# Latent attention: operands split before they are stored, softmax division on ScalarE, and layer 0's memory weights split on VectorE

## The chip, the cores and the metric

One NeuronCore of one Trainium2 chip. The metric is the device time of one execution of the whole kernel in microseconds (us), as a median over several executions. Engines: TensorE (PE, its weight loads PEld), VectorE (DVE), ScalarE (ACT), GpSimd (POOL), and SyncE (SP), which in this kernel only issues DMAs. "Granted clock" is the share of full speed that TensorE was allowed.

## What is computed

A decoder trunk of two layers on 1024 tokens of width 1024, all float32. Each layer is a mixer, a cross-attention into 256 memory tokens and a squared-ReLU MLP, each between two RMS norms and added to the residual. Layer 0's mixer, in which the change lies, computes two groups of heads from one input projection:

```python
def _mla(c_q, c_kv, k_pe, positions, g_q, w_uq, g_kv, w_ukv):      # 8 heads
    q = (_rmsnorm(c_q, g_q) @ w_uq).reshape(B, S, H, 64 + 32)      # rank 256
    kv = (_rmsnorm(c_kv, g_kv) @ w_ukv).reshape(B, S, H, 64 + 64)  # rank 128
    q_pe, k_pe = rope(q[..., 64:]), rope(k_pe)                     # k_pe is shared by the heads
    s = (q_nope @ k_nope.T + q_pe @ k_pe.T) * (64 + 32) ** -0.5    # causal
    o = softmax(s) @ v
...
def _gla(q, k, v, g_lr, r, w_gate, b_gate, g_norm):                # 4 heads, 64 and 128 wide
    # S_t = diag(a_t) S_{t-1} + k_t^T v_t, o_t = q_t S_t, in chunks
    o = _rmsnorm(o, g_norm).reshape(B, S, H * DV)                  # over each head's 128
    return o * silu(r)
...
mix = concat(mla, gla) @ w_out
```

The cross-attention's keys and values come from the memory tokens and four weight matrices of each layer (`xa_w_k`, `xa_w_v`, `xa_w_q`, `xa_w_o`).

## The kernel before

**Products.** Each float32 operand of a matmul is split into a high half, rounded to TensorE's fast format (fp32r), and a low half, the rest; `acc3` adds three products: high by high, high by low, low by high. `split` makes the halves: by default ScalarE copies the high half (line 137), VectorE or, with `lo_eng="pool"`, GpSimd subtracts it from the source for the low half (line 143). `fetch` loads a weight block of 128x1024 into `raw` and splits it into `wh` and `wl`; a `Stream` fetches a list of blocks some blocks ahead.

**Stages.** Layer 0's mixer (`mix0`) has the input projection, then the latent projections, in two groups of four heads (`grp`), then eight token tiles of the gate `r` (`tok`), then the attention. For each group the latent projections compute, feature by feature:
- `qpe`, the rotary part of the four queries (`uq`, evicted by ScalarE at line 1207), which eight DMAs from SBUF to SBUF copy with halves exchanged into `swap` (line 1209); VectorE multiplies both with cosine and sine, GpSimd adds, and four DMAs store the result to `mq` in DRAM (line 1214);
- for both pairs of heads `q` and `k` (lines 1220 and 1223), stored head by head to `mq` and `mk` (lines 1225 and 1226), in plain float32;
- `v` for eight token tiles (line 1234), stored to `mv` for each four tiles (line 1237).

**The attention** sweeps 8 heads by 4 blocks of 256 queries (`seq`). For a step, `scores` computes two tiles of 128 queries: matmuls, the row maximum (VectorE, line 1302), the exponential with its row sum (ScalarE, 1304), the reciprocal and the division (VectorE, 1305 and 1306), into `prob`. `turn` transposes `prob` on TensorE and splits the transposes; `values` multiplies them with V. `head_qk` loads a head's `q` and `k` (three DMAs) into `raw` buffers and splits them, `pair_v` does so for V, ahead of use. Into the gaps between the matmuls the code writes two other streams of work, one after each step: the gated linear attention, a generator (`gla`), chunk by chunk: gate levels `lev`, Gram products `gr`, state update `gS`, output `o`, its norm (lines 1036 to 1042), the transpose `gT` and the store to `gd`; and layer 0's memory stage (`mem_side`), which folds the 32 blocks of cross-attention weights with the memory.

**Order and buffers.** A scheduler writes the order of each engine from the code's order when the kernel is built. Each engine works its list in order, SP too; SP's DMAs take turns on 8 semaphores. Buffers are tiles of fixed pools: 34 of 128x1024 (`u`), 12 for weights, 3 `raw`, 3 `t2`; in PSUM single banks (`p1`) and double banks (`p2`). A buffer is given again when its last reader is done: for a tile that is stored, when the store has landed.

Of the kernel before, what the change touches and what calls it, by code (L numbers as in the profile page):

```python
# [77 lines left out]
class Trunk:  # L78
# [635 lines left out]
    def mem_side(self, l):  # L714
# [7 lines left out]
        W = Stream(self, blocks, 1, "pool")  # L722
# [158 lines left out]
    def mix0(self):  # L881
# [11 lines left out]
        ggla = self.cp.tile([P, P], F32, name="ggla")  # L893
        nc.sync.dma_start(ggla, self.bcast_row(T["g_gla"]))
# [6 lines left out]
        qd, kd = self.dram("mq", [8, 96, S]), self.dram("mk", [8, 64, S])  # L901
        krd, vd = self.dram("mkr", [32, S]), self.dram("mv", [4, P, NT, P])
# [27 lines left out]
        def gla():  # L930
# [6 lines left out]
            for c in range(NT):  # L937
# [99 lines left out]
                nc.vector.tensor_tensor(natural(oc), heads(o[:, :, 0:256]), natural(srg), ALU.mult)  # L1037
                nc.vector.tensor_reduce(stt[:, 0:4], at.rearrange("p r (a b) -> p (r a) b", b=P), AX.X, ALU.add)
                self.rstd(stt[:, 4:8], stt[:, 0:4])
                for hd in range(4):  # L1040
                    w, x = slice(hd * P, (hd + 1) * P), 4 + 2 * (hd % 2) + hd // 2
                    nc.vector.tensor_scalar(oc[:, w], oc[:, w], stt[:, x:x + 1], None, ALU.mult)
# [19 lines left out]
        def head_qk(hd):  # L1062
            res = []
            for a in range(2):
                t = self.raw([P, S], "qk")
                if a:
                    nc.sync.dma_start(t[0:64, :], kd[hd])
                    nc.sync.dma_start(t[64:96, :], krd)
                else:
                    nc.sync.dma_start(t[0:96, :], qd[hd])  # L1070
                h, l = self.parts([96, S], "kq"[1 - a])
                self.split(h, l, t[0:96, :])
                res.append((h, l))
            qk[hd] = res

        def pair_v(pair):
            t = self.raw([P, NT, P], "V")
            nc.sync.dma_start(t.rearrange("p a b -> p (a b)"), vd[pair].rearrange("p a b -> p (a b)"))

            V[pair] = [self.u([P, NT, 2, 64], F32R, "V") for _ in range(2)]  # L1080
            for b, x in enumerate(V[pair]):
                self.split(x[:, :, 0, :], x[:, :, 1, :], t[:, :, 64 * b:64 * b + 64])


        with self.psum(4, 2):
# [56 lines left out]
            nc.sync.dma_start(krd, kr[0:32, :])  # L1142
            del pe, kr, wg, reset, c0
# [52 lines left out]
            for grp in range(2):  # L1196
                wuq = self.fetch(T["w_uq"][grp])

                def uq(t, half):
                    ps = self.p1("uq")  # L1200
                    self.acc3(ps, [(tuple(w[:, t * 256 + k * P:t * 256 + k * P + P] for w in wuq), tuple(x[:, half_cols(half)] for x in qn[k])) for k in range(2)])
                    return ps


                x, y = self.u([P, S], F32, "qpe"), self.u([P, S], F32, "swap")
                for half in range(2):
                    nc.scalar.activation(x[:, half_cols(half)], uq(0, half), AF.Copy, scale=asc)
                for h in range(8):
                    nc.sync.dma_start(y[16 * h:16 * h + 16, :], x[16 * (h ^ 1):16 * (h ^ 1) + 16, :])
                nc.vector.tensor_tensor(x, x, cs, ALU.mult)  # L1210
                nc.vector.tensor_tensor(y, y, sn, ALU.mult)
                nc.gpsimd.tensor_tensor(x, x, y, ALU.add)
                for h in range(4):
                    nc.sync.dma_start(qd[4 * grp + h, 64:96, :], x[32 * h:32 * h + 32, :])
                for pair in range(2 * grp, 2 * grp + 2):
                    q, k = self.u([P, S], F32, "q"), self.u([P, S], F32, "k")
                    w = slice(pair * P, pair * P + P)
                    for half in range(2):
                        c = half_cols(half)
                        nc.scalar.activation(q[:, c], uq(1 + pair % 2, half), AF.Copy, scale=asc)  # L1220
                        ps = self.p1("uk")
                        self.acc3(ps, [(tuple(x[:, w] for x in wkv), tuple(x[:, c] for x in kn))])
                        nc.vector.tensor_copy(k[:, c], ps)
                    for b in range(2):
                        nc.sync.dma_start(qd[2 * pair + b, 0:64, :], q[64 * b:64 * b + 64, :])
                        nc.sync.dma_start(kd[2 * pair + b], k[64 * b:64 * b + 64, :])
                w = slice(512 + grp * 256, 512 + grp * 256 + 256)
                for i in range(NT):
                    if not i % 4:
                        v = self.u([P, 4, 2, P], F32, "v")  # L1230
                    ps = self.p1("V")
                    t = slice(i * P, (i + 1) * P)
                    self.acc3(ps[:, :256], [(tuple(x[:, t] for x in kn), tuple(x[:, w] for x in wkv))])
                    nc.scalar.activation(v[:, i % 4], ps[:, :256].rearrange("p (a b) -> p a b", a=2), AF.Copy)
                    if i % 4 == 3:
                        for a in range(2):
                            nc.sync.dma_start(vd[2 * grp + a][:, i - 3:i + 1, :], v[:, :, a, :])
            del wuq, wkv, qn, kn, x, y, q, k, v, cs, sn
            self.rope = None
            wv = [W.next() for _ in range(4)]  # L1240
            for i in range(NT):
                x = self.t2()
                self.silu(x, tok(i, wv), self.t2())
                v = x.rearrange("p (a b) -> p a b", b=P)
                nc.gpsimd.tensor_tensor(v, v, ggla.unsqueeze(1).broadcast_to([P, 4, P]), ALU.mult)
# [7 lines left out]
            del wv, x, v  # L1253
# [11 lines left out]
        with self.psum(4, 2):  # L1265
# [10 lines left out]
            def scores(hd, r):  # L1276
# [3 lines left out]
                for a in range(2):  # L1280
# [25 lines left out]
                    nc.vector.tensor_scalar(p, p, st[:, 3:4], None, ALU.mult)  # L1306
                    pts.append(p)
                probs[hd, r] = pts

            def turn(hd, r):  # L1310
# [3 lines left out]
                for jp in range(r + 1):  # L1314
# [3 lines left out]
                    for n, (jj, a) in enumerate(cells):  # L1318
                        nc.tensor.transpose(tp[:, n * P:n * P + P], pts[a][:, (2 * jp + jj) * P:(2 * jp + jj + 1) * P], self.ident)
# [7 lines left out]
            def values(hd, r):  # L1327
                xs = probs.pop((hd, r))
                b, pair = hd % 2, hd // 2
                v = V[pair][b]  # L1330
                po = self.p1("pv")
                n = 2 * r + 2
                for j in range(n):
# [37 lines left out]
            values(*seq[-2])  # L1371
            turn(*seq[-1])
# [451 lines left out]
def pack(inputs):  # L1824
# [53 lines left out]
    A["g_gla"] = f["ev_g_gla"]  # L1878
# [62 lines left out]
```

## Time and profile before

| | |
|---|---|
| median of 3 executions | 2979.53 us (2977.46 to 2980.94) |
| profiled execution: its own time, its span | 2979.67 us, 2977.9 us |
| mean granted clock | 0.980 |
| busy share of the span: PE, PEld, DVE, ACT, POOL | 96, 79, 64, 47, 30% |
| DMA | 385.09 MB, mean 129 GB/s |

The span runs from the first to the last recorded instruction; the own time has a little around it. A row of a timeline begins with its start and its length in us, then the engine, the line of the kernel, the operation, output<-inputs with shapes, and a count; in square brackets stands the time for which the engine was idle before it and what ended that. A row of a group ends with its busy time, the mean ns of one, and the idle time before its members by what ended it. Busy shares are means over stages with different limits, so a stage is read from its own stretch.

### The profile page before, as it was taken

To read this page: it belongs to the slowest core of one execution; us is meant where nothing else is said; L and a number is where in the kernel's file an instruction comes from. 1 tells how busy PE (TensorE), PEld (TensorE's weight loads), DVE (VectorE), ACT (ScalarE), POOL (GpSimd) and SP (SyncE) were. 2 spreads that over 40 slices of the span, in tenths; PEclk is the share of its full clock that TensorE was granted. 3 is DMA by queue.
4 is the path that set the end of the run, shared out by engine and by line. 5 is a ranking of instruction groups with operands and counts; after the bars stand their busy time and mean duration, and the time that the engine had idled before them with its cause. 6 is when DMAs were issued, how large, how long until landed. Compare 5 with 4: busy or idle time off the path is not lost. (4 is left out here: it accounts for less than half of the span.)

```text
span 2977.9 us, 37928 instructions
## 1 busy us (share of the span) xinstructions
PE 2846.6 (96%) x14470; PEld 2355.4 (79%) x14470; DVE 1909.4 (64%) x2348; ACT 1402.7 (47%) x2391; POOL 898.2 (30%) x674
## 2 busy tenths in 40 slices
PE   7998999999999999999999999889999999999998
PEld 6777888888887888787867888887788788878776
DVE  4237788754347443799876657887733744458995
ACT  4346666633346455433445565543433655544332
POOL 2204545233330000167050113357533100006723
PEclk9998999999999999999999999999999999999999
DMA  4264544352322333531163345547323233263204
GB/s 160 97 165 147 168 141 148 116 197 71 109 104 90 109 113 136 203 114 64 52 223 96 122 144 178 189 163 251 113 63 121 85 108 112 103 231 111 98 17 142
DMA packets 165222, 385.09 MB, mean 129 GB/s; under 512 B 16748, under 2 KB 66316, under 8 KB 165040
## 3 DMA queue, kind: packets, MB, share of 16 engines
q1 hardware_dynamic: 146608, 349.10, 35.0%
q10 hardware_dynamic: 18432, 33.56, 2.9%
q8 instruction: 114, 1.87, 0.3%
q14 instruction: 68, 0.56, 0.1%
HBM read 267.86 MB, written 113.69 MB: 128 GB/s over the span
## 5 line engine op out<-in xcount | busy, mean ns | idle before, releaser
L143 DVE TENSOR_TENSOR wl<-blk,wh 128x1024 fp32r<-128x1024 f32 x276 | 451.7, 1659 | 320.0 <-ACT wh L137 320.0
L493 POOL TENSOR_TENSOR blk<-blk 128x1024 f32<-128x1024 f32 x80 | 252.4, 3183 | 869.0 <-DVE wl L143 863.5
L137 ACT ACTIVATE wh<-blk 128x1024 fp32r<-128x1024 f32 x276 | 281.8, 1054 | 327.6 <-PE op L561 188.7
L560 PE MATMUL up<-hnh,wh 128*128 128x512 f32 x896 | 356.0, 398 | 9.6 <-ACT hnh L137 5.0
L561 PE MATMUL up<-hnl,wh 128*128 128x512 f32 x896 | 354.5, 396 | 4.8 <-DVE hnl L143 4.8
L562 PE MATMUL up<-hnh,wl 128*128 128x512 f32 x896 | 353.4, 395 | 0.0
L561 PE MATMUL op<-wl,wh 128*128 128x512 f32 x784 | 307.9, 393 | 9.7 <-DVE wl L143 9.6
L560 PE MATMUL op<-wh 128*128 128x512 f32 x784 | 306.3, 395 | 6.2 <-ACT wh L137 6.2
L562 PE MATMUL op<-wh,wl 128*128 128x512 f32 x784 | 306.0, 390 | 0.0
L137 ACT ACTIVATE wh<-raw 128x1024 fp32r<-128x1024 f32 (+1 forms) x163 | 170.6, 1058 | 138.1 <-DMA raw<-hd 25.9
L143 POOL TENSOR_TENSOR wl<-raw,wh 128x1024 fp32r<-128x1024 f32 x66 | 158.9, 2420 | 223.6 <-ACT wh L137 208.3
L560 PEld LDWEIGHTS up<-hnh,wh 128*128 128x128 f32 x896 | 169.1, 189 | 51.3 <-ACT hnh L137 11.4
L561 PEld LDWEIGHTS up<-hnl,wh 128*128 128x128 f32 x896 | 169.3, 189 | 45.5 <-DVE hnl L143 6.3
L562 PEld LDWEIGHTS up<-hnh,wl 128*128 128x128 f32 x896 | 169.3, 189 | 40.1
L143 DVE TENSOR_TENSOR wl<-raw,wh 128x1024 fp32r<-128x1024 f32 (+1 forms) x97 | 126.6, 1315 | 99.7 <-ACT wh L137 99.3
L561 PEld LDWEIGHTS op<-wl,wh 128*128 128x128 f32 x784 | 148.0, 189 | 47.1 <-DVE wl L143 16.4
L560 PEld LDWEIGHTS op<-wh 128*128 128x128 f32 x784 | 149.1, 191 | 39.0 <-ACT wh L137 8.2
L562 PEld LDWEIGHTS op<-wh,wl 128*128 128x128 f32 x784 | 147.8, 188 | 30.5
L187 POOL TENSOR_SCALAR st<-st 128x1 f32<-128x1 f32 x99 | 41.6, 421 | 361.6 <-ACT hn L303 307.4
L306 POOL TENSOR_TENSOR h<-h,hn 128x1024 f32<-128x1024 f32 x47 | 128.4, 2732 | 33.5 <-DVE hn L305 26.2
L673 DVE TENSOR_TENSOR acc<-acc,op 128x512 f32<-128x512 f32 x192 | 123.8, 676 | 4.3 <-PE op L562 4.1
L287 DVE SCALAR_TENSOR_TENSOR hn<-h,st,gain 128x1024 f32<-128x1024 f32 x48 | 101.8, 2122 | 26.1 <-POOL st L188 24.8
(440 smaller groups left out, 6993.5 us busy)
## 6 DMA issues: line engine op xcount, KB each, us to landing
blk<-in_ffn_w_dram SPq DMA_DIRECT2D x120, 512.0 KB, 4.3
h<-h SPq DMA_DIRECT2D x80, 512.0 KB, 4.1
hd<-t ACTq DMA_DIRECT2D x128, 256.0 KB, 2.9
blk<-hd SPq DMA_DIRECT2D x56, 512.0 KB, 4.2
raw<-in_w_in_dram SPq DMA_DIRECT2D x24, 512.0 KB, 4.1
h<-in_x_dram SPq DMA_DIRECT2D x16, 512.0 KB, 6.3
raw<-in_xa_w_k_dram SPq DMA_DIRECT2D x16, 512.0 KB, 3.7
raw<-in_xa_w_v_dram SPq DMA_DIRECT2D x16, 512.0 KB, 3.8
```

The source lines that it names most:

```text
L137: nc.scalar.activation(hi, src, AF.Copy)
L143: e.tensor_tensor(lo, src, hi.bitcast(F32), ALU.subtract)
L187: self.nc.gpsimd.tensor_scalar(dst, src, EPS, None, ALU.add)
L287: nc.vector.scalar_tensor_tensor(hn, h, st[:, 1:2], gpre, ALU.mult, ALU.mult)
L306: nc.gpsimd.tensor_tensor(h, h, t, ALU.add)
L493: eng.tensor_tensor(out, a, b, op)
L560: mm(ps, lh, rh, start=start and not i, stop=False, skip_group_check=True)
L561: mm(ps, lh, rl, start=False, stop=False, skip_group_check=True)
L562: mm(ps, ll, rh, start=False, stop=i == n - 1, skip_group_check=True)
L673: nc.vector.tensor_tensor(dst, dst, ps[i], ALU.add)
```

## The change

Four edits:
1. **Layer 0's memory weights**: the low halves of the 32 blocks are computed on VectorE and not on GpSimd.
2. **Operands split at their source**: `q`, `k`, `v`, the rotary parts and the shared rotary key are split where the projection is evicted, and both halves are stored (`mq`, `mk`, `mkr` and `mv` have twice the size); `q` and `k` in pieces of 512 tokens, `v` of two token tiles. `head_qk` and `pair_v` load the halves straight into `u` tiles, six DMAs for a head and two for a pair, without a split. The rotary products move from VectorE to GpSimd, and behind the group's V tiles.
3. **Division**: `divide` scales `prob` on ScalarE; the code calls it for a step ahead of the next step's `scores`.
4. **Linear attention's norm**: `o` is scaled by the norm and multiplied with the gate in one VectorE instruction for each head, from PSUM; the gain `g_gla` is a scale for each partition at the eviction of `gT` and no longer a product on GpSimd for each of the eight gate tiles.

```diff
-        W = Stream(self, blocks, 1, "pool")
+        W = Stream(self, blocks, 1, "pool" if l else "dve")
...
-                nc.vector.tensor_tensor(natural(oc), heads(o[:, :, 0:256]), natural(srg), ALU.mult)
                 nc.vector.tensor_reduce(stt[:, 0:4], at.rearrange("p r (a b) -> p (r a) b", b=P), AX.X, ALU.add)
                 self.rstd(stt[:, 4:8], stt[:, 0:4])
                 for hd in range(4):
...
-                    nc.vector.tensor_scalar(oc[:, w], oc[:, w], stt[:, x:x + 1], None, ALU.mult)
+                    nc.vector.scalar_tensor_tensor(oc[:, w], o[:, a, p * P:p * P + P], stt[:, x:x + 1], srg[:, w], ALU.mult, ALU.mult)
...
-                    nc.scalar.activation(g, tp, AF.Copy)
+                    nc.scalar.activation(g, tp, AF.Copy, scale=ggla)
...
         def head_qk(hd):
             res = []
             for a in range(2):
-                t = self.raw([P, S], "qk")
-                if a:
-                    nc.sync.dma_start(t[0:64, :], kd[hd])
-                    nc.sync.dma_start(t[64:96, :], krd)
-                else:
-                    nc.sync.dma_start(t[0:96, :], qd[hd])
-                h, l = self.parts([96, S], "kq"[1 - a])
-                self.split(h, l, t[0:96, :])
-                res.append((h, l))
+                res.append(self.parts([96, S], "kq"[1 - a]))
+                for part, t in enumerate(res[a]):
+                    if a:
+                        nc.sync.dma_start(t[0:64, :].bitcast(F32), kd[hd, part])
+                        nc.sync.dma_start(t[64:96, :].bitcast(F32), krd[part])
+                    else:
+                        nc.sync.dma_start(t.bitcast(F32), qd[hd, part])
...
-            V[pair] = [self.u([P, NT, 2, 64], F32R, "V") for _ in range(2)]
-            for b, x in enumerate(V[pair]):
-                self.split(x[:, :, 0, :], x[:, :, 1, :], t[:, :, 64 * b:64 * b + 64])
+            V[pair] = [self.u([P, 4, 2, 2, 64], F32R, "V") for _ in range(2)]
+            for t, src in zip(V[pair], vd[pair]):
+                nc.sync.dma_start(t.rearrange("p a b c d -> p (a b c d)").bitcast(F32), src.rearrange("p a b c d -> p (a b c d)"))
...
-                nc.vector.tensor_tensor(x, x, cs, ALU.mult)
-                nc.vector.tensor_tensor(y, y, sn, ALU.mult)
-                nc.gpsimd.tensor_tensor(x, x, y, ALU.add)
-                for h in range(4):
-                    nc.sync.dma_start(qd[4 * grp + h, 64:96, :], x[32 * h:32 * h + 32, :])
                 for pair in range(2 * grp, 2 * grp + 2):
-                    q, k = self.u([P, S], F32, "q"), self.u([P, S], F32, "k")
...
-                        nc.scalar.activation(q[:, c], uq(1 + pair % 2, half), AF.Copy, scale=asc)
+                        q, k = self.u([P, 2, HALF], F32R, "q"), self.u([P, 2, HALF], F32R, "k")
+                        ps = uq(1 + pair % 2, half)
+                        nc.scalar.activation(q[:, 0], ps, AF.Copy, scale=asc)
+                        nc.vector.scalar_tensor_tensor(q[:, 1], ps, asc, q[:, 0].bitcast(F32), ALU.mult, ALU.subtract)
...
-                        nc.vector.tensor_copy(k[:, c], ps)
-                    for b in range(2):
-                        nc.sync.dma_start(qd[2 * pair + b, 0:64, :], q[64 * b:64 * b + 64, :])
-                        nc.sync.dma_start(kd[2 * pair + b], k[64 * b:64 * b + 64, :])
+                        self.split(k[:, 0], k[:, 1], ps)
+                        for b in range(2):
+                            for t, dst in ((q, qd), (k, kd)):
+                                nc.sync.dma_start(dst[2 * pair + b, :, 0:64, c].rearrange("r p t -> p r t"), t[64 * b:64 * b + 64].bitcast(F32))
...
-                    nc.scalar.activation(v[:, i % 4], ps[:, :256].rearrange("p (a b) -> p a b", a=2), AF.Copy)
-                    if i % 4 == 3:
+                    self.split(v[:, i % 2, :, :, 0, :], v[:, i % 2, :, :, 1, :], ps[:, :256].rearrange("p (a b c) -> p a b c", a=2, b=2))
+                    if i % 2:
...
+                nc.gpsimd.tensor_tensor(x, x, cs, ALU.mult)
+                nc.gpsimd.tensor_tensor(y, y, sn, ALU.mult)
+                nc.gpsimd.tensor_tensor(x, x, y, ALU.add)
+                xs = self.parts([P, S], "qpe")
+                self.split(*xs, x, lo_eng="pool")
+                for part, t in enumerate(xs):
+                    for h in range(4):
+                        nc.sync.dma_start(qd[4 * grp + h, part, 64:96, :], t[32 * h:32 * h + 32, :].bitcast(F32))
...
-                nc.gpsimd.tensor_tensor(v, v, ggla.unsqueeze(1).broadcast_to([P, 4, P]), ALU.mult)
...
-                    nc.vector.tensor_scalar(p, p, st[:, 3:4], None, ALU.mult)
-                    pts.append(p)
+                    pts.append((p, st))
...
+            def divide(hd, r):
+
+                for p, st in probs[hd, r]:
+                    nc.scalar.activation(p, p, AF.Copy, scale=st[:, 3:4])
...
+                if n:
+                    divide(*seq[n - 1])
                 scores(hd, r)
```

How the order of the engines changes, at three places.

**ScalarE, latent projections of the second group.** `uq`, `uk` and `V` are PSUM banks; in brackets stand the semaphores for which a row waits (DMAHW0 to DMAHW7 are the DMAs' eight). Before:

```order
L1207 ACTIVATE qpe_1492<-uq_1494 128x512 [waits PE_49]
L1207 ACTIVATE qpe_1492<-uq_1502 128x512 [waits PE_49]
L1220 ACTIVATE q_1525<-uq_1527 128x512 [waits DMAHW5_49,DMAHW7_49,PE_49,Activation_49]
L1220 ACTIVATE q_1525<-uq_1540 128x512 [waits PE_49]
L1220 ACTIVATE q_1557<-uq_1559 128x512 [waits DMAHW2_49,DMAHW3_49,DMAHW1_49,DMAHW4_49,DMAHW0_49,DMAHW6_49,PE_49,Pool_49]
L1220 ACTIVATE q_1557<-uq_1572 128x512 [waits PE_49]
L1234 ACTIVATE v_1589<-V_1590 128x256 [waits DMAHW3_49,DMAHW4_49,DVE_49,PE_49]
```

and now:

```order
L1202 ACTIVATE qpe_1539<-uq_1541 128x512 [waits DMAHW1_49,DMAHW3_49,DVE_49,PE_49]
L1202 ACTIVATE qpe_1539<-uq_1549 128x512 [waits PE_49]
L1211 ACTIVATE q_1565<-uq_1567 128x512 [waits DMAHW4_49,DMAHW6_49,DVE_49,PE_49]
L137 ACTIVATE k_1566<-uk_1576 128x512 [waits DMAHW5_49,DMAHW7_49,DVE_49,PE_49]
L1211 ACTIVATE q_1586<-uq_1588 128x512 [waits DMAHW0_49,DMAHW1_49,DVE_49,PE_49]
L137 ACTIVATE k_1587<-uk_1597 128x512 [waits DMAHW2_49,DMAHW3_49,DVE_49,PE_49]
L1211 ACTIVATE q_1607<-uq_1609 128x512 [waits DMAHW4_49,DMAHW5_49,DVE_49,PE_49]
L137 ACTIVATE k_1608<-uk_1618 128x512 [waits DMAHW6_49,DMAHW7_49,DVE_49,PE_49]
L1211 ACTIVATE q_1628<-uq_1630 128x512 [waits DMAHW1_49,DMAHW2_49,DMAHW0_49,DMAHW3_49,PE_49,Pool_49]
L137 ACTIVATE k_1629<-uk_1639 128x512 [waits DMAHW6_49,DMAHW5_49,DMAHW7_49,DMAHW4_49,PE_49]
```

Each eviction of `q` and of `k` in the second group now takes a buffer of its own and waits for DMAs that read its old content, the last two for the stores of the first group's rotary halves.

**SP, from the last stores of the latent projections to the attention's first loads** (`grd` is the gate's tile, `cm` the causal mask, `G` the linear attention's first chunk, `gain` and `mem` belong to the memory stage). Before:

```order
L1237 DMA mv<-v 128x4x128 x2
L1214 DMA mq<-qpe 32x1024 x4
L1237 DMA mv<-v 128x4x128 x2
L1070 DMA qk<-mq 96x1024
L1067 DMA qk<-mk 64x1024
L1068 DMA qk<-mkr 32x1024
L1268 DMA cm<-in_cmask_dram 128x512
L720 DMA gain<-in_g_mem_dram 128x1024
L1246 DMA grd<-t_1647 128x512
L940 DMA G<-gld 128x1024
```

and now:

```order
L1230 DMA mv<-v 128x2x256 x8
L1238 DMA mq<-qpeh 32x1024 x4
L1238 DMA mq<-qpel 32x1024 x4
L1246 DMA grd<-t_1736 128x512
L1067 DMA qh<-mq 96x1024
L1067 DMA ql<-mq 96x1024
L1064 DMA kh<-mk 64x1024
L1065 DMA kh<-mkr 32x1024
L1064 DMA kl<-mk 64x1024
L1246 DMA grd<-t_1769 128x512
L1065 DMA kl<-mkr 32x1024
L936 DMA G<-gld 128x1024
```

A group's transfers from `swap` to the last store grow from 24 to 40 (8 swaps, 16 of `q` and `k`, 8 of `v`, 8 of the rotary halves). A head's six loads and two gate tiles' stores now stand between the last of them and `G`.

**VectorE, a late chunk of the linear attention in the attention** (at 420 us of the trace before; `t` is the chunk's output, `stg` its norm, `kt` the keys' halves, `sta` the maxima and sums of a step's rows, `pv` the values' bank). Before:

```order
L963 TENSOR_TENSOR lev<-lev,G 128x256 x4
L1042 TENSOR_SCALAR t_3962<-t_3962,stg 128x128
L1032 SCALAR_TENSOR_TENSOR gS<-gS,ekq,su 128x128 x2
L143 TENSOR_TENSOR kt<-kt 128x512
L1042 TENSOR_SCALAR t_3962<-t_3962,stg 128x128 x3
L1302 TENSOR_REDUCE sta<-sc 128x1 x2
L1305 RECIPROCAL sta<-sta 128x1
L1306 TENSOR_SCALAR prob<-prob,sta 128x896
L1344 TENSOR_TENSOR t_4024<-pv,t_4024 64x256
L1305 RECIPROCAL sta<-sta 128x1
L1306 TENSOR_SCALAR prob<-prob,sta 128x1024
```

and now:

```order
L959 TENSOR_TENSOR lev<-lev,G 128x256 x4
L1038 SCALAR_TENSOR_TENSOR t_4015<-o,stg,vr 128x128 x4
L1028 SCALAR_TENSOR_TENSOR gS<-gS,ekq,su 128x128 x2
L143 TENSOR_TENSOR kt<-kt 128x512
L143 TENSOR_TENSOR wl<-raw,wh 128x1024
L1302 TENSOR_REDUCE sta<-sc 128x1
L143 TENSOR_TENSOR wl<-raw,wh 128x1024
L1348 TENSOR_TENSOR t_4076<-pv,t_4076 64x256
L1302 TENSOR_REDUCE sta<-sc 128x1
L1305 RECIPROCAL sta<-sta 128x1 x2
```

The norm's scalings are fused with the gate, the divisions have left the list, and two low halves of memory weights (`wl`) stand ahead of a step's row maxima. On ScalarE, where the divisions now are, each stands behind the other exponential of its step or behind the first of the next. TensorE's list is the same but for neighbours that change places.

More of the change, by code (lines that the diff above doesn't have):

```diff
@@ L892, in mix0 @@
         wg, reset = c0[:, 0:256], c0[:, 256:384]
-        ggla = self.cp.tile([P, P], F32, name="ggla")
-        nc.sync.dma_start(ggla, self.bcast_row(T["g_gla"]))
+        ggla = self.const("g_gla")
         ones = self.cp.tile([P, P], F32, name="ones")
@@ L899, in mix0 @@
         gld, gvd, grd = self.dram("gld", [NT, P, 4, 256]), self.dram("gvd", [NT, P, 512]), self.dram("grd", [NT, P, 512])
-        qd, kd = self.dram("mq", [8, 96, S]), self.dram("mk", [8, 64, S])
-        krd, vd = self.dram("mkr", [32, S]), self.dram("mv", [4, P, NT, P])
+        qd, kd = self.dram("mq", [8, 2, 96, S]), self.dram("mk", [8, 2, 64, S])
+        krd, vd = self.dram("mkr", [2, 32, S]), self.dram("mv", [4, 2, P, 4, 2, 2, 64])
         gd = self.dram("gd", [NT, P, 512])
@@ L1141, in mix0 @@
             nc.gpsimd.tensor_tensor(kr[0:32, :], pe[0:32, :], kr[0:32, :], ALU.add)
-            nc.sync.dma_start(krd, kr[0:32, :])
-            del pe, kr, wg, reset, c0
+            krs = self.parts([32, S], "kr")
+            self.split(*krs, kr[0:32, :])
+            for part, t in enumerate(krs):
+                nc.sync.dma_start(krd[part], t.bitcast(F32))
+            del pe, kr, krs, wg, reset, c0
             def tok(i, ws):
@@ L1219, in mix0 @@
                         c = half_cols(half)
-                        nc.scalar.activation(q[:, c], uq(1 + pair % 2, half), AF.Copy, scale=asc)
+                        q, k = self.u([P, 2, HALF], F32R, "q"), self.u([P, 2, HALF], F32R, "k")
+                        ps = uq(1 + pair % 2, half)
+                        nc.scalar.activation(q[:, 0], ps, AF.Copy, scale=asc)
+                        nc.vector.scalar_tensor_tensor(q[:, 1], ps, asc, q[:, 0].bitcast(F32), ALU.mult, ALU.subtract)
                         ps = self.p1("uk")
                         self.acc3(ps, [(tuple(x[:, w] for x in wkv), tuple(x[:, c] for x in kn))])
-                        nc.vector.tensor_copy(k[:, c], ps)
-                    for b in range(2):
-                        nc.sync.dma_start(qd[2 * pair + b, 0:64, :], q[64 * b:64 * b + 64, :])
-                        nc.sync.dma_start(kd[2 * pair + b], k[64 * b:64 * b + 64, :])
+                        self.split(k[:, 0], k[:, 1], ps)
+                        for b in range(2):
+                            for t, dst in ((q, qd), (k, kd)):
+                                nc.sync.dma_start(dst[2 * pair + b, :, 0:64, c].rearrange("r p t -> p r t"), t[64 * b:64 * b + 64].bitcast(F32))
+                del q, k
                 w = slice(512 + grp * 256, 512 + grp * 256 + 256)
                 for i in range(NT):
-                    if not i % 4:
-                        v = self.u([P, 4, 2, P], F32, "v")
+                    if not i % 2:
+                        v = self.u([P, 2, 2, 2, 2, 64], F32R, "v")
                     ps = self.p1("V")
@@ L1252, in mix0 @@
                     next(linear)
-            del wv, x, v
+            del wv, x
         self.hn = [None, None]
@@ L1329, in values @@
                 b, pair = hd % 2, hd // 2
-                v = V[pair][b]
+                v = [t[:, j, b] for t in V[pair] for j in range(4)]
                 po = self.p1("pv")
@@ L1371, in mix0 @@
             values(*seq[-2])
+            divide(*seq[-1])
             turn(*seq[-1])
@@ L1877, in pack @@
     A["g_q"], A["g_kv"] = cols(f["ev_g_q"][0]), cols(f["ev_g_kv"][0])
-    A["g_gla"] = f["ev_g_gla"]
+    A["g_gla"] = cols(f["ev_g_gla"][0])
     A["w_out0"] = km(f["ev_w_out"][0])
```

19 lines of the change are left out of this document (8 added, 11 removed).

## The prediction

> **What bounds the kernel now.** I read the page first, then the trace in stretches of 50 us, then, for each stretch in which TensorE loses time, what its waits end on. The page says that TensorE is the bound of the whole:
>
> ```profile
> PE 2846.6 (96%) x14470; PEld 2355.4 (79%) x14470; DVE 1909.4 (64%) x2348; ACT 1402.7 (47%) x2391; POOL 898.2 (30%) x674
> ```
>
> So a lighter engine is worth only what TensorE now waits for it, and what it loses to the lower clock that follows such waits. Nearly all of the edit lies between 175 and 600 us: the latent projections (175 to 258) and the attention with the linear attention and layer 0's memory in its gaps (258 to 600). There the stretches read (us: PE, PEld, DVE, ACT, POOL busy; granted clock; DMA share; GB/s):
>
> ```profile
> 275.00:325.00 50.00, 45.85 (x375) 41.94 (x376) 41.71 (x72) 28.41 (x58) 26.86 (x25) 0.93 0.39 122
> 325.00:375.00 50.00, 48.83 (x408) 43.52 (x407) 37.39 (x69) 33.31 (x64) 27.31 (x24) 1.00 0.52 164
> 375.00:425.00 50.00, 45.99 (x377) 40.67 (x375) 38.49 (x63) 29.61 (x59) 24.63 (x24) 0.97 0.49 161
> 425.00:475.00 50.00, 46.11 (x428) 41.74 (x429) 42.53 (x82) 32.81 (x69) 21.76 (x26) 0.90 0.43 137
> 475.00:525.00 50.00, 48.61 (x416) 43.43 (x415) 40.91 (x83) 33.51 (x71) 20.64 (x23) 1.00 0.45 144
> 525.00:575.00 50.00, 48.22 (x378) 42.62 (x376) 36.35 (x68) 28.37 (x62) 14.82 (x18) 0.93 0.25 81
> ```
>
> TensorE is idle for 16.4 us in these 300 (50 minus its busy time, summed), and the clock takes 13.5 more at most (50 times one minus the clock, summed: 3.5, 0, 1.5, 5, 0, 3.5). That 30 us is the whole pot of the attention. Most of the idle time is three waits. The timeline of the last one, and the heads of the other two:
>
> ```profile
> 420.25 4.71 POOL L143 TENSOR_TENSOR wl<-raw,wh 128x1024 fp32r<-128x1024 f32 x2 [2.83 <-ACT wh L137]
> 420.30 5.05 DVE L1042 TENSOR_SCALAR t<-t,stg 128x128 f32<-128x128 f32 x3
> 426.38 1.01 ACT L1304 ACTIVATE prob<-sc,sta 128x896 f32<-128x896 f32 x1 [5.26 <-DVE sta L1302]
> 427.53 1.23 PE L927 MATMUL gr<-lev 64*128 64x128 f32 x8 [3.22 <-ACT prob L1304]
> ...
> 379.30 0.86 PE L927 MATMUL gr<-lev 64*128 64x128 f32 x8 [3.16 <-ACT prob L1304]
> ...
> 279.24 5.03 DVE L963 TENSOR_TENSOR lev<-lev,G 128x256 f32<-128x256 f32 x4
> 284.42 1.22 PE L927 MATMUL gr<-lev 64*128 64x128 f32 x8 [4.15 <-DVE lev L963]
> ```
>
> Three VectorE multiplications of 128 elements take 5.05 us, just as long as GpSimd works on two low halves of memory weights (4.71 us). Behind them stand the row maxima, behind these the exponentials, and a Gram matmul waits for the bank that the exponential frees. At 279 four level products of 256 elements take 5.03 in the same way. The three waits make 10.5 of the 16.4 us, and the stretches that hold them have 10 of the 13.5 us of lost clock.
>
> **The change, part by part.** Durations are of one profiled execution: span 2977.9 us, its own time 2979.67, the median of the runs 2979.53. The sum is made on 2979.67, 0.1 above the median.
>
> The costs in the attention go by these groups (busy us, mean ns of one):
>
> ```profile
> L1306 DVE TENSOR_SCALAR prob<-prob,sta 128x256 f32<-128x256 f32 (+3 forms) x64 | 51.2, 810 | 1.3
> L1042 DVE TENSOR_SCALAR t<-t,stg 128x128 f32<-128x128 f32 x32 | 17.9, 639 | 1.2 <-POOL stg L188 1.2
> L143 DVE TENSOR_TENSOR wl<-raw,wh 128x1024 fp32r<-128x1024 f32 (+1 forms) x13 | 17.2, 1326 | 11.0 <-ACT wh L137 11.0
> L143 DVE TENSOR_TENSOR ql<-qk,qh 96x1024 fp32r<-96x1024 f32 x8 | 9.7, 1217 | 13.2 <-ACT qh L137 13.2
> L143 DVE TENSOR_TENSOR kl<-qk,kh 96x1024 fp32r<-96x1024 f32 x8 | 9.7, 1214 | 0.0
> L1037 DVE TENSOR_TENSOR t<-o,vr 128x512 f32<-128x512 f32 x8 | 5.5, 682 | 3.5 <-ACT at L1036 3.5
> L1304 ACT ACTIVATE prob<-sc,sta 128x256 f32<-128x256 f32 (+3 forms) x64 | 48.2, 755 | 41.7 <-DVE sta L1302 36.1 <-DVE sta L1305 5.1
> L137 ACT ACTIVATE qh<-qk 96x1024 fp32r<-96x1024 f32 x8 | 8.4, 1050 | 11.8 <-DMA qk<-mq 11.8
> L137 ACT ACTIVATE kh<-qk 96x1024 fp32r<-96x1024 f32 x8 | 8.4, 1049 | 0.2 <-DMA qk<-mkr 0.2
> L143 POOL TENSOR_TENSOR wl<-raw,wh 128x1024 fp32r<-128x1024 f32 x32 | 75.9, 2382 | 109.0 <-ACT wh L137 98.8 <-PE pT L1319 10.2
> ```
>
> 1. Division to ScalarE: VectorE loses 51.2 us; ScalarE gains 64 copies, which no row shows from SBUF to SBUF in place; the nearest are the exponentials of the same 64 shapes, 48.2 us. In the order a copy stands behind the other exponential of its step, or the first one of the next, well ahead of its transposes; it needs one reciprocal of VectorE's. If that is late, the exponentials behind the copy are too (the second rival).
> 2. Operands that arrive split: 19.4 us off VectorE and 16.8 off ScalarE, and the smaller V splits with them. Six loads for each head instead of three; they are issued a head ahead, at a DMA share under 0.52, and I cost them at nothing. If SP were held up, the next head's scores would be late.
> 3. Linear attention's norm: eight multiplications (5.5) go, 32 scalings become fused ones that read PSUM: between 5.5 us (L1037's work in 32 pieces) and the 17.9 of now; I take 9. The bank of `o` is held until the norm is known; 36 to 48 memory matmuls stand behind it on TensorE.
> 4. Layer 0's memory weights: GpSimd loses 32 low halves, 75.9 us, and with them every long operation in the attention; VectorE gains 32 of 1326 ns, 42.4 us.
>
> VectorE ends 43 us lighter (51.2 + 19.4 + 5.5 + 9 less 42.4), ScalarE 31 heavier (48.2 less 16.8), before what the end of the collisions gives. On the path: of the three waits (10.5 us) I keep 0.7 each, since two low halves of 1.3 us now stand where the blocked ones stood: 8.4 gained. Their clock: of 10 us I take 8. Of the other 5.9 us of idle time and 3.5 of clock, a bit over a third: 3.6. Together 20 us; the bounds are the pot, 30, and 6, if the two low halves in the queue cost as much as the collision did.
>
> 5. The price: the latent stage. Every operand is stored twice. SP's rows there, and the DMA's:
>
> ```profile
> 179.82 5.05 SPq L1209 DMA_DIRECT2D swap<-qpe  x8
> 184.97 0.54 SPq L1225 DMA_DIRECT2D mq<-q  x1
> ...
> 192.31 0.78 SPq L1237 DMA_DIRECT2D mv<-v  x1
> 193.19 3.25 SPq L1214 DMA_DIRECT2D mq<-qpe  x4
> 196.48 1.76 SPq L1237 DMA_DIRECT2D mv<-v  x3
> ```
> ```profile
> mq<-q SPq DMA_DIRECT2D x8, 256.0 KB, 4.0
> mq<-qpe SPq DMA_DIRECT2D x8, 128.0 KB, 2.7
> G<-gld SPq DMA_DIRECT2D x2, 512.0 KB, 6.1
> ```
> ```profile
> 180.00:218.00 38.00, 37.42 (x184) 31.04 (x183) 14.56 (x15) 14.44 (x30) 6.08 (x3) 1.00 0.82 203
> 218.00:230.00 12.00, 12.00 (x54) 9.67 (x53) 2.95 (x3) 3.98 (x5) 0.05 (x1) 1.00 0.99 304
> 230.00:258.00 28.00, 23.87 (x173) 19.15 (x171) 17.71 (x27) 15.77 (x30) 14.37 (x17) 0.92 0.41 140
> ```
> ```profile
> 204.86 0.40 PE L1151 MATMUL tok<-wh,hnh 128*128 128x512 f32 x1
> 238.38 0.71 PE L927 MATMUL gr<-G 64*128 64x128 f32 x8
> 256.15 2.08 PE L927 MATMUL gr<-lev 64*128 64x128 f32 x16 [4.13 <-ACT t L397]
> 258.16 0.58 PE L1296 MATMUL sc<-kh,qh 96*128 96x256 f32 x1
> ```
>
> Today the DMA stands at a share of 0.82 from 180 to 218 us and of 0.99 from there to 230, yet TensorE does not feel it, since a group takes few buffers. In the new order the second group's evictions wait for the first group's stores: the last of them (`k_1629`) for the eight stores of the rotary halves, the 40th store of the group. When does that land? Eight swaps 5.05 us; q and k 0.92 each (eight from 184.97 to 192.31), sixteen: 14.7; eight of v at 0.59 (1.76 for three): 4.7; eight rotary ones at 0.81 (3.25 for four): 6.5. From 179.8 that ends at 210.8, landing (2.7 us) at 213.5. Behind it come that tile's two halves (0.7 us on VectorE by L1037, about as much on ScalarE) and the V tiles that found no bank: the tokens begin near 217 instead of 204.86, 12 us late. The same 31 us again for group two, to 242, then the eight loads ahead of `G`'s in SP's order, at the 0.54 to 0.78 of the single rows above, and `G`'s load lands near 253; TensorE asks for it at 238.4 + 12, so 2 to 3 us more. Against that, the wait of 4.13 at 256 may shrink, while the gaps cost clock: 1 us net. First scores 13 us late; the bounds: 0, if the stores drain as fast as they come, and 30: the extra stores (16 of 256 KB for q and k, 8 for v, 8 of 128 KB, 7.3 MB) at 203 GB/s over a share of 0.82, 248 GB/s, with no idle DMA time used. The added evictions there are covered by VectorE's 14.6 and ScalarE's 14.4 busy us of 38, the rotary products by GpSimd's 6.1.
>
> 6. `g_gla` as a scale, and the shared key's split: eight GpSimd products less, two small operations and a store more, beside TensorE's full rows: nothing.
>
> Sum: 2979.7 + 13 - 20 = 2973.
>
> At part 1 a rule speaks against the change. The Trainium skill, ScalarE: Activation LUTs, section Rules for kernel authors, says to multiply on VectorE and not on ScalarE, since VectorE is faster per element. No run here shows the new copy; if it were a loss, the division would be it, which is the second rival below.
>
> **The rivals.**
> *The stores drain faster.* At 218 to 230 the DMA moved 304 GB/s; the first group's 40 transfers (7.86 MB) would take 26 us and not 31, the tokens would begin 7 us late: 2967. For it speaks that row, against it that it is mostly loads. The Trainium skill, DMA: Bandwidth & Descriptors, section Where 436 GB/s comes from, puts the limit between HBM and SBUF at about 358 GB/s for a core; by that the 7.86 MB take 22 us, some 3 us late, an estimate of 2963.
> *ScalarE becomes the one that is late.* It goes from about 31 to 35 busy us in 50; an exponential behind a copy of up to 1 us holds its bank longer. If half of the gain is lost so: 2979.7 + 13 - 10 = 2983. Against it: an exponential (0.75 us) mostly stands between, in which the reciprocal can come.
> *The stores come out on the path, slower.* SP is one queue in order: head 0's operands, `G`, `V` and the memory's weights stand behind the stores. If the 30 us are paid in full and the attention gains its 20: 2990. It decides once the extra delay passes 20 us; against it speaks the share of 0.41 from 230 to 258, room for 16 us.
> That the edit does not take place can't be: the order shows each move.
>
> **How the numbers follow.** Likeliest, 2973 (own range 2965 to 2981): 0.42. Faster stores, 2967: 0.18. ScalarE late, 2983: 0.20. Stores on the path, 2990: 0.20. A measurement here tells 0.2%, 6 us, from nothing. Faster by that: 0.25 of the first, most of the second, 0.43; same: 0.14, 0.03 and 0.12 of the first three, 0.29; slower: 0.28. The range of 8 in 10 reaches to the centres of both outer cases and a little over: 2960 to 2991.
>
> **What would show it.** In the new profile: TensorE idle by 10 to 15 us between 187 and 218, ended by evictions that wait for DMA; first scores near 271; no VectorE row of 128 elements over 1 us in the attention, no Gram wait over 2 us; clock 0.97 or more from 275 to 575; the attention from first score to the output projection 20 us shorter. Wrong if the evictions never wait for a store, or if the Gram waits stay at 3 us.

## The result: slower, 2999.36 us

The changed kernel takes 2999.36 us in the median of four executions against 2980.24 before: a ratio of 1.0062 (1.0042 to 1.0082), slower by 0.6% and above the range. One execution of it at a clock of 0.75 (3506.18 us) and one of e3 below (7139.13 us) stand far off; they count in these medians (2998.47 and 2968.02 without them) and in no ratio. The span of the profile grew from 2977.9 to 2996.7 us. Four starts on TensorE show where:

| us | before | changed |
|---|---|---|
| first scores (`sc`) begin | 258.2 | 276.4 |
| from there to the output projection's first product | 329.4 | 317.7 |
| from there to layer 0's first MLP product | 289.9 | 293.0 |
| from there to the end | 2100.4 | 2109.7 |

So +18.2 ahead of the attention, -11.7 in it, +3.1 behind it and +9.3 in the rest. The page's line, then the attention's slices as they were shown of before (columns as there):

```profile
PE 2854.8 (95%) x14470; PEld 2359.8 (79%) x14470; DVE 1869.0 (62%) x2305; ACT 1432.3 (48%) x2442; POOL 823.5 (27%) x640
```
```profile
275.00:325.00 50.00, 43.39 (x353) 38.19 (x350) 37.59 (x72) 34.81 (x75) 12.68 (x23) 0.90 0.59 173
325.00:375.00 50.00, 49.50 (x421) 45.07 (x420) 30.84 (x60) 37.66 (x74) 9.26 (x18) 1.00 0.66 204
375.00:425.00 50.00, 49.80 (x420) 44.48 (x419) 33.09 (x62) 38.18 (x76) 8.69 (x16) 1.00 0.63 182
425.00:475.00 50.00, 48.55 (x407) 43.76 (x406) 34.76 (x70) 31.28 (x64) 13.19 (x24) 0.97 0.52 156
475.00:525.00 50.00, 47.45 (x454) 41.30 (x454) 36.74 (x75) 39.82 (x84) 8.87 (x16) 1.00 0.56 166
525.00:575.00 50.00, 50.00 (x417) 45.00 (x417) 33.32 (x69) 37.69 (x79) 9.36 (x18) 1.00 0.40 120
```

GpSimd fell from 23 to 10 busy us of 50 in the mean, and the mean clock rose from 0.955 to 0.978. TensorE still idles 11.3 us of the 300 (16.4 before). (The slices stand at the same times, but the changed kernel's attention begins 18 us later in them.) The latent stage, TensorE and the DMA from 187 to 218 us, before and then changed, then ScalarE's evictions in the changed one:

```profile
187.00:218.00 31.00, 30.43 (x154) 25.40 (x153) 12.48 (x12) 11.83 (x27) 6.08 (x3) 1.00 0.87 226
```
```profile
187.00:218.00 31.00, 21.56 (x91) 17.01 (x92) 13.94 (x26) 11.92 (x26) 8.86 (x4) 0.88 0.85 242
```
```profile
200.86 0.60 ACT L1211 ACTIVATE q<-uq 128x512 fp32r<-128x512 f32 x1 [1.62 <-DMA mq<-q]
202.64 0.60 ACT L137 ACTIVATE k<-uk 128x512 fp32r<-128x512 f32 x1 [1.18 <-DMA mk<-k]
...
213.15 0.60 ACT L137 ACTIVATE k<-uk 128x512 fp32r<-128x512 f32 x1 [2.19 <-DMA mq<-qpel]
```
```profile
217.90 0.63 PE L1146 MATMUL tok<-wh,hnh 128*128 128x512 f32 x1
257.47 1.23 PE L923 MATMUL gr<-G 64*128 64x128 f32 x8 [4.79 <-DMA G<-gld]
276.37 0.58 PE L1296 MATMUL sc<-kh,qh 96*128 96x256 f32 x1
299.59 0.79 PE L1296 MATMUL sc<-kh,qh 96*128 96x512 f32 x1 [3.73 <-ACT prob L1304]
```

Evictions wait for stores, the last for the rotary halves, and TensorE idles 9.4 us of the 31 at a lower clock; the tokens begin at 217.90, 13.0 us late. `G` comes another 4.79 us late, and from the tokens to the first scores 58.5 us pass and not 53.3, at a mean clock of 0.91 (0.96 before). At 299.59 scores wait for a bank that an exponential frees; before, scores had no wait of that length. VectorE's rows say why the exponential is late:

```profile
294.31 1.23 DVE L143 TENSOR_TENSOR wl<-raw,wh 128x1024 fp32r<-128x1024 f32 x1
295.46 1.95 DVE L959 TENSOR_TENSOR lev<-lev,G 128x256 f32<-128x256 f32 x3
297.33 1.08 DVE L1302 TENSOR_REDUCE sta<-sc 128x1 f32<-128x896 f32 x1
```

Its row maximum stands behind a low half of a memory weight, which VectorE now computes, and behind three level products. In the groups, the copy and the fused norm:

```profile
L1312 ACT ACTIVATE prob<-prob,sta 128x256 f32<-128x256 f32 (+3 forms) x64 | 49.3, 791 | 5.8 <-DVE sta L1305 5.8
```
```profile
L1038 DVE SCALAR_TENSOR_TENSOR t<-o,stg,vr 128x128 f32<-128x128 f32 x32 | 9.0, 340 | 0.1
```

### The profile page after: what moved, and what is told of

It reads as the page before. It is cut to its first block, busy times and chain, and to the rows that moved or that the text cites. A ratio compares the mean times of both kernels' runs of the same rounds, so it can differ in the third digit from the quotient of the medians.

```text
span 2996.7 us, 38081 instructions
## 1 busy us (share of the span) xinstructions
PE 2854.8 (95%) x14470; PEld 2359.8 (79%) x14470; DVE 1869.0 (62%) x2305; ACT 1432.3 (48%) x2442; POOL 823.5 (27%) x640
## 5 line engine op out<-in xcount | busy, mean ns | idle before, releaser
L143 DVE TENSOR_TENSOR wl<-raw,wh 128x1024 fp32r<-128x1024 f32 x129 | 169.5, 1322 | 104.7 <-ACT wh L137 101.9
L561 PEld LDWEIGHTS op<-wl,wh 128*128 128x128 f32 x784 | 147.7, 188 | 47.1 <-DVE wl L143 16.5
L143 POOL TENSOR_TENSOR wl<-raw,wh 128x1024 fp32r<-128x1024 f32 x34 | 84.9, 2509 | 141.5 <-ACT wh L137 138.9
```

Source lines behind the costliest of these rows:

```text
L143: e.tensor_tensor(lo, src, hi.bitcast(F32), ALU.subtract)
L561: mm(ps, lh, rl, start=False, stop=False, skip_group_check=True)
```

## The experiments

All kernels as medians, with the ratio to runs of before on the same chip, and the same stages from the starts in the trace:

| kernel | us | ratio (95%) | first scores | attention | to the MLP | rest |
|---|---|---|---|---|---|---|
| e1 memory weights | 2971.53 | 0.9980 (0.9972 to 0.9989) | 256.5 | 318.8 | 291.0 | 2102.8 |
| e2 division | 2999.38 | 1.0073 (1.0060 to 1.0086) | 258.4 | 340.9 | 291.1 | 2105.2 |
| e3 all but the split | 2968.33 | 0.9968 (0.9959 to 0.9977) | 256.5 | 311.6 | 293.7 | 2106.5 |
| e4 the split alone | 3003.43 | 1.0085 (1.0072 to 1.0098) | 281.0 | 324.7 | 290.9 | 2108.7 |
| e5 fewer bytes | 2973.76 | 0.9988 (0.9978 to 0.9998) | 256.6 | 313.1 | 293.7 | 2106.2 |
| e6 changed, again | 2995.85 | 1.0068 (1.0054 to 1.0082) | 276.0 | 319.1 | 293.5 | 2108.9 |
| e7 memory, norm | 2978.66 | 1.0002 (0.9994 to 1.0011) | 256.5 | 328.1 | 293.0 | 2101.0 |
| e8 as e3, layer 1 too | 2947.45 | 0.9905 (0.9891 to 0.9918) | 254.8 | 312.2 | 292.8 | 2084.9 |
| e9 memory, division | 2980.45 | 1.0006 (0.9998 to 1.0015) | 254.9 | 325.1 | 290.7 | 2107.3 |
| e10 as e9, layer 1 too | 2962.31 | 0.9947 (0.9934 to 0.9960) | 257.7 | 323.9 | 290.7 | 2088.1 |
| e11 quarter halves | 2960.44 | 0.9941 (0.9926 to 0.9956) | 253.5 | 322.0 | 290.3 | 2089.1 |
| e12 short GpSimd | 2957.53 | 0.9928 (0.9915 to 0.9942) | 254.3 | 315.5 | 296.2 | 2088.9 |

**e1 to e4: the parts.** e1 is edit 1 alone, e2 edit 3, e4 edit 2, e3 edits 1, 3 and 4.

> Before, with one line of the change: layer 0's memory weights' low halves on VectorE. Theory 1 (the split at the source is what costs; the rest gains): the latent stage as before (first scores near 258 us), the Gram waits of 3.2 to 4.2 us gone, attention 5 to 10 us shorter, so 2970 to 2976. Theory 2 (moving work onto VectorE and ScalarE costs at the attention's end, and the gains come from operands that arrive split): the 42 us more on VectorE make the row maxima late, 2980 to 2986.

> Before, with the division alone moved to ScalarE. Theory 1: VectorE 51 us lighter, but the waits behind GpSimd's low halves stay, 2975 to 2980. Theory 2: the copies make the exponentials late, 2981 to 2988. In both the price of the copy is read here: between 0.4 and 1.1 us by the exponentials' rows.

> The changed kernel without the split at the source: memory weights on VectorE, division on ScalarE and the linear attention's new norm, with q, k and v stored once and split at the load as before. Theory 1: tokens begin at 205 us and first scores at 258 as before, the attention is 10 to 20 us shorter, 2960 to 2970. Theory 2: VectorE and ScalarE carry the splits as well as the new work, the attention gains nothing, 2976 to 2985. Layer 1's linear part, 9.6 us later in the changed kernel by its own waits: as before if it comes from the split's larger stores, 5 to 10 us longer if any other order brings it.

> Before, with the split at the source alone. Theory 1: tokens begin near 218 us and first scores near 276, the attention gains less than 8 us, since GpSimd's low halves stay, so 2990 to 3005. Theory 2: the attention gains its 9 to 15 us here too, 2982 to 2988.

Theory 1 holds for e1, e3 and e4 in their times: without the split, first scores come at 256.5, with it alone at 281.0. (In e1 one Gram wait, 4.72 us at 282.94, stays, behind level products that now queue with two low halves.) The attention is 311.6 us in e3, 17.8 less than before, and 317.7 in the changed kernel: beside the other edits the split gains nothing there, it takes 6.1 us back, and it costs 18 to 23 us ahead of it. From e3 to the changed kernel the span grows by 28.4 us. Behind the attention e3 too takes longer than before (3.8 us to the MLP and 6.1 in the rest), though it stores no more bytes: of the two forecasts for layer 1, that any other order brings its loss is the one that held. But e2 is slower than even theory 2 had it: 2999.4, 21 us above before, of which 11.5 in the attention. Its copies are cheap (0.79 us). The timeline of e2:

```profile
276.97 7.36 POOL L143 TENSOR_TENSOR wl<-raw,wh 128x1024 fp32r<-128x1024 f32 x3
...
278.15 6.46 DVE L963 TENSOR_TENSOR lev<-lev,G 128x256 f32<-128x256 f32 x3
...
286.52 1.21 DVE L1302 TENSOR_REDUCE sta<-sc 128x1 f32<-128x1024 f32 x1
...
288.12 0.58 PE L149 MATMUL kt<-mth,wh 128*128 128x256 f32 x1 [8.60 <-DVE t L1348]
```

Three level products, of which one alone takes 0.41 us, take 6.46 beside three GpSimd low halves, and TensorE waits 8.60. The groups from 256 to 600 us, level products in before, then level products and the norm's scalings in e2 (before, 639 ns), then the divisions in e1 (before, 810 ns):

```profile
L963 DVE TENSOR_TENSOR lev<-lev,G 128x256 f32<-128x256 f32 x49 | 24.7, 545 | 0.8 <-ACT lev L962 0.8
```
```profile
L963 DVE TENSOR_TENSOR lev<-lev,G 128x256 f32<-128x256 f32 x49 | 32.8, 712 | 6.9 <-ACT lev L962 6.8
L1042 DVE TENSOR_SCALAR t<-t,stg 128x128 f32<-128x128 f32 x32 | 23.4, 823 | 1.2 <-POOL stg L188 1.2
```
```profile
L1306 DVE TENSOR_SCALAR prob<-prob,sta 128x256 f32<-128x256 f32 (+3 forms) x64 | 35.4, 562 | 0.9
```

VectorE was not short of time (235 busy us of the attention's 341; 265 of 329 before). In e1, where GpSimd has no low halves beside them, the 64 divisions take 15.8 us less than before: so much blocking they had taken, and they have slack. In e2 they are gone, and level products and scalings, which stand on the chain, take 13.6 us more than before. That the block moved from the ones to the others is how these sums are read here; the division loses on e1 too (e9 below), where GpSimd's low halves are gone, so the block is not all of its price.

**e5, e6: the stores, and layer 1.** e5 is the changed kernel with only the high halves of `q`, `k` and the rotary parts stored, and loaded twice; it leaves the low parts of the scores out. The edit for `q` and `k`:

```diff
-nc.sync.dma_start(dst[2 * pair + b, :, 0:64, c]...
+nc.sync.dma_start(dst[2 * pair + b, 0, 0:64, c], t[64 * b:64 * b + 64, 0].bitcast(F32))
```

> The changed kernel without the stores of the low halves of q, k and the rotary parts (the loads read the high half twice, so the low parts of the scores are left out): a group's stores fall from 7.3 MB to 4.7 MB, the number of transfers from 40 to 36. If the bytes of the stores set the latent stage's delay: tokens begin near 207 us (before 204.9, changed kernel 217.9), first scores near 262, and the whole gains 10 to 15 us on the changed kernel. If SP's number of transfers or the wait of each eviction for its own buffer sets it: tokens still near 214 to 217.

> The changed kernel once more, for the stretch of layer 1 that it does not touch: between the linear part's start and 80 us later it took 89.5 us where the kernel before took 80.0. If that belongs to the kernel, it is 88 to 91 again; if it is a matter of one execution (the value load landed after 8.0 us where 5.5 before), 80 to 86. The whole 2996 to 3002.

Two starts in e5, then the stores of `q` between 174 and 260 us in the changed kernel and in e5:

```profile
207.48 0.39 PE L1146 MATMUL tok<-wh,hnh 128*128 128x512 f32 x1
256.64 0.39 PE L1296 MATMUL sc<-kh,qh 96*128 96x256 f32 x1
```
```profile
mq<-q SPq DMA_DIRECT2D x16, 256.0 KB, 3.9
```
```profile
mq<-q SPq DMA_DIRECT2D x16, 128.0 KB, 2.4
```

First scores come 19.7 us earlier than in the changed kernel, and the whole gains 22 us on e6 and 26 on the first measurement, more than the 10 to 15 of its forecast. The first group's sixteen stores of `q` and `k` are as many in both; at half the bytes SP issues them in 10.2 us and not in 15.5. So the bytes of the stores set the delay (or their rows of 2 KB, which were halved with them), and not the number of transfers.

e6 repeats each stage of the first profile within 1.5 us. From ScalarE's third `row` operation (line 1598, in the changed kernel 1605) to the first `wk` product of layer 1 it took 88.1 us, where the first profile took 90.2 and before 81.4: between the two forecasts, with the same four waits over 1 us, so most of the loss belongs to the kernel. And the rest is 2101.0 to 2107.3 us in the kernels without the larger stores and with layer 1 as in before (2100.4), so a new order alone can cost some of it. One cause is seen: the value load `v` of layer 1's first chunk (before, then changed):

```profile
DMA to landing us min/median/max: 5.5/5.5/5.5
```
```profile
DMA to landing us min/median/max: 8.0/8.0/8.0
```

ScalarE waits for it, VectorE for ScalarE, and TensorE idles 2.48 us at 1796.41 (2.50 in e6), where before has no such wait. It landed after 8.0 us again in e6 and 8.1 in e4, after 5.3 in e5, which has the same buffers in DRAM and fewer stores, and after 5.4 to 5.8 in all the kernels without the split. What carries 1500 us further is open.

**e7, e9: does the norm or the division pay?** e7 is edits 1 and 4, e9 edits 1 and 3.

> Memory weights on VectorE and the linear attention's new norm, the division left on VectorE. Theory now: the division pays only where no long GpSimd work blocks VectorE, and then little, so this stands between the memory weights alone (2971.5) and those three together (2968.3): 2968 to 2972. Rival: the division is a loss there too, hidden by the norm's gain: 2960 to 2966.

> Memory weights on VectorE and division on ScalarE, the linear attention's norm as before. Memory weights alone gave 2971.5, with the norm 2978.7, with norm and division 2968.3; the division alone 2999.4. If the norm is a loss of some 7 us by itself (it holds the bank of the output until the norm is known, and the scores wait 3.7 us for one): 2960 to 2966, with no wait over 2 us ahead of scores near 280 us. If it is a loss only beside divisions on VectorE: 2967 to 2973.

Neither held. On e1 (2971.5) the norm costs 7.1 us, the division 8.9, and both together nothing: 3.2 less, with intervals that overlap. Parts do not add here; each writes another order. In e7 scores wait 3.56 us at 281.67 for a norm's instruction on VectorE, as the prediction's part 3 had it for the memory's matmuls behind the bank. In e9 TensorE waits 4.16 us at 280.22 and 2.26 at 330.47 for the addition that frees `pv`'s bank. The second:

```profile
327.27 1.08 ACT L137 ACTIVATE wh<-raw 128x1024 fp32r<-128x1024 f32 x1
...
328.88 1.21 DVE L143 TENSOR_TENSOR wl<-raw,wh 128x1024 fp32r<-128x1024 f32 x1
...
330.00 0.41 DVE L1348 TENSOR_TENSOR t<-pv,t 64x256 f32<-64x256 f32 x1
...
330.47 0.80 PE L149 MATMUL vo<-wh,vt 128*128 128x512 f32 x1 [2.26 <-DVE t L1348]
```

A weight's halves stand ahead of that addition. Why the order with both edits avoids such places wasn't tried.

**e8, e10: layer 1's memory weights too.** `W = Stream(self, blocks, 1, "dve")`, in e3 and in e9.

> The kernel without the split at the source (memory weights, division, norm), with layer 1's memory weights on VectorE too. In layer 1 each chunk has a wait of about 3 us behind four scalings that VectorE does in over 1 us each while GpSimd works on low halves. Theory now (blocked VectorE instructions on the chain are what these waits are): five such waits go with their clock, 15 to 25 us, 2943 to 2953. Rival: VectorE is nearly full there (32 to 36 busy us of 40), and 42 us more of it end on the path: 2970 to 2985.

> As the run before, with layer 1's memory weights on VectorE too, which gave 21 us with the norm (2947.5): 2940 to 2946 if the norm is a loss by itself, 2946 to 2952 otherwise.

e8 is the fastest kernel, 30 us under before, within the first forecast; in the spans it has 21.6 us less than e3 behind the first MLP product. e10, at 2962.3, lies above both of its forecasts, which went with those of e9; but layer 1's gain comes again, 19.2 us on e9 in the rest. The scalings of layer 1's linear part, as a group in before and in e8, then 100 us of that part in each:

```profile
L1762 DVE TENSOR_SCALAR nm<-nm,stm 128x256 f32<-128x256 f32 x32 | 40.3, 1319 | 0.1
```
```profile
L1762 DVE TENSOR_SCALAR nm<-nm,stm 128x256 f32<-128x256 f32 x32 | 11.1, 411 | 0.0
```
```profile
1860.00:1960.00 100.00, 88.71 (x662) 86.18 (x660) 87.97 (x192) 55.55 (x96) 38.33 (x24) 0.93 0.54 184
```
```profile
1862.00:1962.00 100.00, 97.42 (x764) 93.81 (x763) 97.09 (x222) 63.20 (x109) 11.12 (x14) 1.00 0.62 206
```

VectorE is busy 97 us of 100 and still TensorE runs better than beside a VectorE at 88, whose busy time holds the blocked instructions: work that fills VectorE cost less here than work that stops it.

**e11, e12: the length of a GpSimd instruction.**

```diff
+            n = src.shape[1] // 4
+            for q in range(4):
+                c = slice(n * q, n * q + n)
+                nc.gpsimd.tensor_tensor(lo[:, c], src[:, c], hi[:, c].bitcast(F32), ALU.subtract)
```

> Before, with each low half on GpSimd cut into four instructions of a quarter of the columns (both layers' memories and two other places). If VectorE is kept out for the length of one GpSimd instruction and then gets its turn: blocked instructions last 0.9 us and less instead of 1.3 to 2.5, the Gram waits of 3.2 to 4.2 us shrink to under 2, so 2962 to 2974. If the two only share a bandwidth, in proportion to what they move: the same waits, and GpSimd's extra instructions beside them, 2976 to 2990.

> The fastest kernel so far (memory weights of both layers on VectorE, division, norm: 2947.5) with three of GpSimd's remaining long products cut into quarters: the two skip products of each mLSTM chunk (3.2 us each) and the residual's addition (2.7 us). If the length of one GpSimd instruction is what VectorE waits for: the additions of a chunk (1.2 us alone, up to 3.4 beside a skip product) shrink, and the whole gains 2 to 10 us, 2938 to 2945. If GpSimd's work there is not on the chain, or its extra instructions make its square roots later: 2946 to 2955.

e11 leaves GpSimd its work, and more of it, in pieces, and gains 19 us, a little more than the first forecast; the second, a shared bandwidth, is out. Its group, and a collision like that of before at 420:

```profile
L148 POOL TENSOR_TENSOR wl<-raw,wh 128x256 fp32r<-128x256 f32 x128 | 95.5, 779 | 92.7 <-ACT wh L137 81.7 <-PE su L1033 10.9
```
```profile
407.29 2.86 DVE L1047 TENSOR_SCALAR t<-t,stg 128x128 f32<-128x128 f32 x4
407.93 5.05 POOL L148 TENSOR_TENSOR wl<-raw,wh 128x256 fp32r<-128x256 f32 x7
...
412.34 0.72 PE L932 MATMUL gr<-lev 64*128 64x128 f32 x8 [1.01 <-ACT prob L1309]
```

Four scalings beside such pieces take 2.86 us where three took 5.05, and the Gram wait is 1.01, not 3.22. In the attention the longest scaling takes 1.11 us (2.64 before) and the longest level product 1.20 (2.56), though the mean of the level products is no lower (589 ns, 545 before). So VectorE gets its turn between two GpSimd instructions: a single block is shorter, not the sum of them. The Trainium skill, SBUF — State Buffer, section SBUF: two separate sides, says that VectorE and GpSimd share a port pair as an exclusive lock for a whole instruction; e11 agrees (the shorter the lock, the shorter the wait). e12 shortens VectorE's products beside the skip connections; the additions, which its forecast meant, take as long as before, but wait 29.3 us for GpSimd and not 15.8, and the kernel is 10 us slower than e8, slower than both forecasts (e8, then e12):

```profile
L1711 DVE TENSOR_TENSOR hT<-hT,zg 128x1024 f32<-128x1024 f32 x8 | 19.8, 2473 | 3.5 <-DMA zg<-zd 3.5
L1712 DVE TENSOR_TENSOR hT<-hT,xg 128x1024 f32<-128x1024 f32 x8 | 9.8, 1225 | 15.8 <-POOL xg L1705 15.7
```
```profile
L1717 DVE TENSOR_TENSOR hT<-hT,zg 128x1024 f32<-128x1024 f32 x8 | 13.0, 1620 | 1.2 <-DMA zg<-zd 1.2
L1718 DVE TENSOR_TENSOR hT<-hT,xg 128x1024 f32<-128x1024 f32 x8 | 9.8, 1225 | 29.3 <-POOL xg L1711 29.3
```

Of the 10 us the spans put 4.0 in the rest, where these rows stand, 3.3 in the attention and 3.4 behind it; what costs there was not followed. So pieces are seen to serve in e11, where the longest waits were for blocked VectorE instructions, and not in e12, where VectorE waits for GpSimd's end.

## Why the prediction was wrong

It forecast 2973 from +13 and -20; the spans give +18.2, -11.7, and +12.4 for which it had no term. Two steps failed: the price of the double stores was sized too low, and what lies behind the attention was put at nothing without a reason.

- *The price of the stores* (part 5, and part 2's "I cost them at nothing"): the mechanism was right, the size was not. Tokens came at 217.90 (forecast near 217). The 1 us for all behind them was too little, 5.2 came: `G`'s load landed after 8.0 us (6.1 in before's row) and TensorE waited 4.79 for it and not 2 to 3, and the clock from the tokens to the first scores was 0.91. And the price does not end at the first scores: from e3 to the changed kernel the split costs 19.9 us up to there, 6.1 in the attention and 28.4 in the whole span, where 13 was forecast. With fewer bytes stored (e5), 22 to 26 us of the whole come back, so the bytes are the cause of most of it. The rival with stores fully on the path was nearest; its 30 us were close for the split as a whole, but it had them all ahead of the attention.
- *Behind the attention* (no term): 12.4 us. e3 has 9.9 of them without the larger stores, so most belongs to the new order; in layer 1 one late load is seen, the rest is waits of 1 to 4 us with their clock, and what sets those is open.
- *The gain of the attention* (parts 1 to 4): no Gram product of the attention waits over 2 us, no scaling of the norm lasts over 0.36 us and the clock is 0.98 in the mean of the six slices, all as forecast. But from the first scores to the output projection TensorE idles 16.5 us where 21.5 were lost before: the sum counted the old waits and no new one, and 3.73 came at 299.59, behind a low half on VectorE. Its other bound, 6, was for such a queue. Without the split the attention gained 17.8, near the 20; that is in part luck, since the parts do not add as the sum has them: edit 1 alone gained 10.6, with the norm 1.3, with the division 4.3. The division was costed by its copies (0.79 us, as bounded), yet alone it lost 21 us.
- *The collisions* (waits): right, and larger than the edit used: e8 gains some 20 us on e3 by ending the same blocking in layer 1, and e11 19 in the whole kernel with GpSimd's work left where it was.
- *ScalarE late* (rival two): not seen. ScalarE stands at 31 to 40 busy us of 50, and in e3, with the division and the old splits, the attention is shortest.
- *The chances*: by the shares that it gives, faster comes to 0.40 and slower to 0.31, not 0.43 and 0.28.

## What to carry to other kernels

Before work is moved off a full engine, look at which of its instructions stand beside a long instruction of the engine that blocks it: an instruction with slack may be what catches the block, and taking it away may put the chain there. Remove the block itself first, by moving the long instructions or cutting them. Storing a product twice to save a split that nobody waits for bought nothing here, and the bytes cost time where buffers are given back by stores, and again where the next loads queue behind them. Run each part alone and in pairs, since a scheduler makes another order of every one, and give the stages that the edit does not touch a term or a wider range.

## What the runs showed of the hardware

A VectorE scaling of 128x128 that takes 0.28 us (the median in before) took up to 2.64 us beside GpSimd instructions of 2.4 us, and up to 1.11 beside pieces of 0.78 (e11). A ScalarE copy with a scale cost as much (0.79 us) as VectorE's multiplication had in before (0.81), of which part was blocking: in e11 the same multiplications took 0.61, in e1 0.56. So the rule of the Trainium skill (ScalarE: Activation LUTs, Rules for kernel authors), to multiply on VectorE as the faster for each element, agrees with these rows in float32; but the 0.2 us did not decide, since with the copies on ScalarE e3 is faster than e7 and e9 slower than e1. Stores of 256 KB from 64 partitions landed after 3.9 us and their halves after 2.4 (medians of `q` in the changed kernel and e5), and SP's own time for one rose with them. And the first value load of layer 1 (512 KB, 1500 us behind the changed stage) took 2.5 us longer in all three profiles with the larger stores than in before.
